# Strassen's scheme for the gates and the output product of a transformer block, in one item loop with the hidden layer

## The chip, the cores and the metric

One core of a Trainium2 chip. The metric is the device time of one execution, in microseconds; the median of several runs is given. The engines are TensorE (PE in the rows, with PEld for its weight loads), VectorE (DVE), ScalarE (ACT), GpSimd (POOL) and SyncE (SP), which here issues nearly all DMA transfers, in order.

## The reference

One block over 2048 latent tokens with 1024 channels, all in fp32. What matters here, cut down:

```python
q, k, v, p, g = split(modulate(layernorm(x)) @ w_in)
attn_d = banded_attention(q, k, v, ...) @ w_attn_branch
pooled = multiscale_pool(p)          # 4 groups of 128 channels, windows 2, 4, 8, 16, minus the token
pool_d = einsum('blgc,gcd->blgd', pooled, w_pool) * pool_scale
g_attn, g_pool = g[..., :1024], g[..., 1024:]
merged = sigmoid(g_attn) * attn_d + sigmoid(g_pool) * pool_d
x = layernorm(ALPHA * x + g1 * (merged @ w_out), ln1_g, ln1_b)
h = square(relu(modulate(layernorm(x)) @ w_mlp_in)) @ w_mlp_out
out = layernorm(ALPHA * x + g2 * h, ln2_g, ln2_b)
```

## The kernel before

fp32 products are made of three fp32r products: each operand is split into a rounded high part (ScalarE, line 59) and the rest (VectorE, line 62), and high x high, high x low and low x high are summed in PSUM. The channels u of the normalised, modulated input and the attention output lie channel-major in DRAM (`u_scr`, `a_scr`). TensorE's order is written by hand in attention and in both layers of the MLP; everything else, and all of TensorE's work in the stretch between them, is ordered by a scheduler that follows a simulated timeline.

Stages: the start and attention, up to 872 us; at its end the high and low parts of u for the first 1024 tokens are loaded (`load_u`) and two of the four pooling groups are computed between attention's products (`early_pool`). Then a stretch that runs once for each half of the tokens (`for c in range(2)`), to 1763 us: pooling channels (`p_group`: 8 x 3 x 3 matmuls of 344 columns), window sums on GpSimd (`p_finish`), the pooling branch's gate and map (`pool_gate`), the attention branch's gate (`sa`), the branch map with the merge (`mg`), and the output product token-major (`out_mm`: 256 columns each, 24 matmuls), with LN1 (`ln_affine`), a second normalisation (`ln1_u`) and the transposes back to channels (`u2_half`). u2_half also forms the four sums of half-size blocks that the hidden layer needs and stores seven planes in `us_scr`. All full products here take 24 matmuls of 512 columns for 128 channels x 512 tokens. 16 column pieces of w_ada are multiplied along the way (`ada_load`, `ada_sum`).

The hidden layer (`Pair`, from 1763 us) uses Strassen's scheme in Winograd's form: a 256-channel x 1024-token piece is cut 2 x 2, its 4-step sums are made on GpSimd, and seven products of half-size blocks (ORDER, 12 matmuls each) stand for eight. `step` splits the weights seven products ahead, `l_fill` splits the planes of the tokens. The outputs are combined with additions from PSUM on VectorE and four more sums on GpSimd, and go to DRAM (`hs_scr`) as planes for the second layer (`w2_fill`, `h_fill`, `prod2`, from 2393 us), which works in the same way and ends with LN2.

## Time and profile before

| | us |
|---|---|
| median of 3 runs | 3035.51 (3033.14 to 3039.31) |
| the profiled execution | 3039.96 |
| its span, first to last instruction | 3038.2 |
| start and attention | 872.3 |
| pooling, gates, branch map, output product, LN1 | 890.5 |
| hidden layer | 617.7 |
| between the layers | 12.5 |
| second layer and LN2 | 645.2 |

Of the span TensorE is busy for 2909.0 us, VectorE for 1819.1, ScalarE for 1369.1 and GpSimd for 1380.6. The stages are read off the first and last matmuls on each stage's PSUM tiles. In the rows below, "idle before" is the time in which the engine sat idle just before instructions of that group, and behind the arrow stands what ended most of it.

### The profile page before, as it was taken

To read this page: it belongs to the slowest core of one execution; us is meant where nothing else is said; L and a number is where in the kernel's file an instruction comes from. 1 tells how busy PE (TensorE), PEld (TensorE's weight loads), DVE (VectorE), ACT (ScalarE), POOL (GpSimd) and SP (SyncE) were. 2 spreads that over 40 slices of the span, in tenths; PEclk is the share of its full clock that TensorE was granted. 3 is DMA by queue.
4 is the path that set the end of the run, shared out by engine and by line. 5 is a ranking of instruction groups with operands and counts; after the bars stand their busy time and mean duration, and the time that the engine had idled before them with its cause. 6 is when DMAs were issued, how large, how long until landed. Compare 5 with 4: busy or idle time off the path is not lost. (4 is left out here: it accounts for less than half of the span.)

```text
span 3038.2 us, 42601 instructions
## 1 busy us (share of the span) xinstructions
PE 2909.0 (96%) x15336; PEld 2481.3 (82%) x15336; DVE 1819.1 (60%) x3201; ACT 1369.1 (45%) x2462; POOL 1380.6 (45%) x1638
## 2 busy tenths in 40 slices
PE   8899999999899999899999779999999799999998
PEld 5789989998888888888889668888888587888886
DVE  5577877877875444742144775557555453556675
ACT  3477767777741131432121455556555332333342
POOL 1867777777540014423032556657665240123244
PEclk9999999999999999999999889999999899999999
DMA  7111111112234433342122475547554684566563
GB/s 255 35 32 37 32 37 31 38 42 61 67 100 144 127 125 111 112 144 78 56 97 84 141 263 161 153 149 222 156 153 124 246 308 153 187 215 218 196 209 108
DMA packets 343015, 395.38 MB, mean 130 GB/s; under 512 B 16785, under 2 KB 277009, under 8 KB 341010
## 3 DMA queue, kind: packets, MB, share of 16 engines
q1 hardware_dynamic: 342802, 392.64, 40.5%
q8 instruction: 121, 1.98, 0.3%
q14 instruction: 92, 0.75, 0.1%
HBM read 275.13 MB, written 117.44 MB: 129 GB/s over the span
## 5 line engine op out<-in xcount | busy, mean ns | idle before, releaser
L1220 PE MATMUL ps_y<-La,R 128*128 128x512 f32 x2688 | 619.4, 393 | 25.8 <-ACT R L59 12.1
L1220 PEld LDWEIGHTS ps_y<-La,R 128*128 128x128 f32 x2688 | 508.9, 190 | 136.4 <-ACT La L59 13.7
L1039 PE MATMUL ps_h<-La,R 128*128 128x512 f32 x2112 | 485.2, 390 | 0.3 <-ACT cx L1044 0.3
L1039 PEld LDWEIGHTS ps_h<-La,R 128*128 128x128 f32 x2112 | 397.2, 188 | 83.3 <-ACT cx L1044 0.7
L62 DVE TENSOR_TENSOR R<-hraw,R 128x512 fp32r<-128x512 f32 x224 | 198.0, 890 | 150.7 <-ACT R L59 150.2
L59 ACT CAST R<-hraw 128x512 fp32r<-128x512 f32 x224 | 137.6, 621 | 281.3 <-PE ps_y L1220 272.9
L62 DVE TENSOR_TENSOR pl<-ps_pt,ph 128x512 fp32r<-128x512 f32 x312 | 212.5, 686 | 70.5 <-ACT ph L59 68.6
L465 POOL TENSOR_SCALAR s<-s,sm 128x640 f32<-128x640 f32 (+1 forms) x256 | 201.6, 795 | 103.0 <-DVE sm L464 53.9
L462 ACT ACTIVATE s<-s,sm 128x641 f32<-128x641 f32 (+1 forms) x256 | 209.8, 820 | 70.2 <-DVE sm L456 69.8
L456 DVE CUSTOM_DVE_ANT_0 s<-ps_s,mask,nsink 128x640 f32<-128x640 f32 (+1 forms) x256 | 211.5, 863 | 29.8 <-PE ps_s L451 29.7
L59 ACT CAST ph<-ps_pt 128x512 fp32r<-128x512 f32 x312 | 179.3, 580 | 109.3 <-PE ps_pt L486 106.0
L861 POOL TENSOR_TENSOR sa<-sa,m 128x512 f32<-128x512 f32 x32 | 57.1, 1805 | 374.5 <-DVE sa L860 374.5
L486 PE MATMUL ps_pt<-ident,s 128*128 128x128 f32 x1248 | 189.7, 274 | 12.4 <-DVE pl L62 8.2
L62 DVE TENSOR_TENSOR R<-sraw,R 128x512 fp32r<-128x512 f32 x160 | 146.3, 917 | 77.3 <-ACT R L59 76.8
L59 ACT CAST wh<-raw 128x2048 fp32r<-128x2048 f32 (+1 forms) x38 | 67.0, 1771 | 276.1 <-DMA raw<-w_in 73.6
L486 PEld LDWEIGHTS ps_pt<-ident,s 128*128 128x128 f32 x1248 | 151.6, 141 | 43.1 <-DVE pl L62 11.3
L62 DVE TENSOR_TENSOR wl<-raw,wh 128x2048 fp32r<-128x2048 f32 (+1 forms) x38 | 86.3, 2274 | 159.5 <-ACT wh L59 159.5
L59 ACT CAST R<-sraw 128x512 fp32r<-128x512 f32 x160 | 98.9, 621 | 155.2 <-PE ps_h L1039 97.5
L1039 PE MATMUL ps_h<-Lb,R 128*128 128x512 f32 x576 | 139.5, 396 | 25.4 <-ACT Lb L59 21.9
L1039 PEld LDWEIGHTS ps_h<-Lb,R 128*128 128x128 f32 x576 | 109.8, 191 | 49.7 <-ACT Lb L59 22.3
L66 PE MATMUL ps_out<-wh,mg 128*128 128x256 f32 x512 | 143.1, 281 | 0.0
L67 PE MATMUL ps_out<-wl,mg 128*128 128x256 f32 x512 | 142.8, 280 | 0.0
(264 smaller groups left out, 7098.4 us busy)
## 6 DMA issues: line engine op xcount, KB each, us to landing
hraw<-hs_scr SPq DMA_DIRECT2D x112, 512.0 KB, 4.0
w<-w_mlp_out SPq DMA_DIRECT2D x72, 512.0 KB, 5.4
sraw<-w_mlp_in SPq DMA_DIRECT2D x64, 512.0 KB, 6.3
hs_scr<-s SPq DMA_DIRECT2D x96, 256.0 KB, 4.6
raw<-w_in SPq DMA_DIRECT2D x19, 1024.0 KB, 5.5
raw<-w_ada SPq DMA_DIRECT2D x16, 1024.0 KB, 5.3
rw<-us_scr SPq DMA_DIRECT2D x14, 1024.0 KB, 5.4
raw<-u_scr SPq DMA_DIRECT2D x8, 1032.0 KB, 5.5
```

The lines of the kernel that those rows point to most:

```text
L59: act.copy(hi, src)
L62: (lo_eng or dve).tensor_tensor(lo, src, hi.bitcast(F32), ALU.subtract)
L66: pe.matmul(ps, sh, mh, start=first, stop=False)
L67: pe.matmul(ps, sh, ml, start=False, stop=False)
L456: dve.tensor_tensor_reduce(out=s[:, 0:n], in0=pieces[z][2], in1=mk[z], op0=ALU.add, op1=ALU.min, scale=-1.0 / math.sqrt(HD), scalar=nsink[ ...
L462: act.activation(s[:, 0:n + 1], s[:, 0:n + 1], AF.Exp, bias=sm[:, 0, j:j + 1], scale=-1.0, accum_out=sm[:, 1, j:j + 1])
L465: pool.tensor_scalar(s[:, 0:n], s[:, 0:n], sm[:, 2, j:j + 1], 1.0, ALU.mult, ALU.mult)
L486: pe.transpose(pt[:, c:c + P], self.s.probs[2 * z + j][:, o:o + P], ident)
L861: pool.tensor_tensor(s, s, m0[j][:, a:a + m], ALU.add)
L1039: pe.matmul(ps, a, b, start=p in (1, 6, 5) and k == 0 and i == 0, stop=k == 3 and i == 2, skip_group_check=p not in (1, 6, 5))
L1220: pe.matmul(ps, a, b, start=n == 0 and z == 0, stop=n == 15 and z == 2)
```

## The change

- **Pooling first.** All six remaining pooling groups of both halves are computed straight after attention, in an order of TensorE written by hand, and the pooled map times `pool_scale` goes to DRAM (`pd_scr`, `p_out`). `load_u` also forms four sums of u's half-size blocks in place on GpSimd (`act_sums`) and stores them (`us1`); the other three planes are read from `u_scr`.
- **Items.** Branch map, gates, output product and hidden layer are classes with the same methods, run in one loop whose order of products is written out: 8 `BranchCols` (plain products, to `ab_scr`), 16 `GateCols` (256 channels of one gate for one half of the tokens: seven products, sigmoid, multiplication with the loaded branch, and in the second of a pair the sum of both and the planes of the merged tensor to `ms_scr`), 8 `Rows` (the output product of 256 tokens, seven products of 512 columns, residual, LN1 in the first four), and 32 `HiddenCols`. Token-side planes of the next stage are loaded and split during the items ahead of it (`Stage.fill`).
- **LN1.** For the first half of the tokens it is done at the end of the item; for the second the sums go to DRAM and come back during the hidden layer of the first half (`ln1_late`). The transposes (`turn_pair`) stand in TensorE's order six to nine products behind.
- **Weights.** w_out times the gate g1 is formed on VectorE and stored as seven planes (`wo_scr`). The modulation's weights are multiplied on ScalarE and summed on VectorE.
- The second layer takes 1 MB tiles of the hidden planes in two buffers and splits its weight planes in halves.

```diff
+    def act_sums(v, sums, c, kk, e):
+        v = v.rearrange("p k (b r t) -> p k r b t", r=2, t=P)
+        a11, a12, a21, a22 = v[:, 0, 0], v[:, 1, 0], v[:, 0, 1], v[:, 1, 1]
+        e.tensor_tensor(a21, a11, a21, ALU.subtract)
+        e.tensor_tensor(a22, a22, a21, ALU.subtract)
+        e.tensor_tensor(a12, a12, a22, ALU.subtract)
+        e.tensor_tensor(a11, a11, a22, ALU.add)
+        for p, t in ((5, a11), (6, a22), (7, a21), (3, a12)):
+            sp.dma_start(sums[c][:, SPL[p], kk].rearrange("p (b t) -> p b t", t=P), t)
...
+            act_sums(raw[:, :, 8 * sums:8 * sums + CH], us1, sums, kk, pool)
...
+    def p_out(c, g, pooled):
+        (ph, pl), (wh, wl) = pooled
+        for jj in range(2):
+            j = 2 * g + jj
+            o = plp.tile([P, CH], F32, name="pdo", tag="pdo", bufs=2)
+            cc = slice(jj * P, (jj + 1) * P)
+            for a, n in HALF:
+                pd = ps2("ps_pd")
+                mm3(pd, (wh[:, cc], wl[:, cc]), (ph[:, a:a + n], pl[:, a:a + n]), True, True)
+                dve.tensor_scalar(o[:, a:a + n], pd, pscale[:, j:j + 1], None, ALU.mult)
+            for r in range(2):
...
+    pw = pool_w(2)
+    fin = [p_finish(early[0], 0, 0)]
+    groups = [(0, 2), (0, 3)] + [(1, g) for g in range(4)]
+    outs = [(0, 0)]
+    uu = uu0
+    for i, (c, g) in enumerate(groups):
+        if (c, g) == (1, 0):
+            uu = []
+            run(load_u(RA, CH - 8, uu, sums=1))
+        nw = pool_w(groups[i + 1][1]) if i + 1 < len(groups) else None
+        pt = p_group(uu, c, g, pw)
+        pw = nw
+        p_out(*outs.pop(0), fin.pop(0))
+        if i == 0:
+            fin.append(p_finish(early[1], 0, 1))
+            p_out(0, 1, fin.pop(0))
+        fin.append(p_finish(pt, c, g))
+        outs.append((c, g))
+    p_out(*outs.pop(0), fin.pop(0))
+    plx.close()
     ptx.close()
-    rpx.close()
...
+    rring = mpa.ring(6 * 4096, name="R")
...
+    rawring = mb.ring(3 * 8192, name="sraw")
+    rwring = mb.ring(3 * 2048, name="rw")
+    string = mb.ring(14 * 2048, name="st")
+    ldring = gp_[0].ring(4 * 2048, name="ld")
+    sring = gp_[0].ring(4 * 2048, name="s")
...
+    class Stage:
+        def __init__(self, src, L=None):
+            self.src, self.L = src, L or {}
+        def fill(self, p):
+            if p in self.L:
+                return
+            self.L[p] = []
+            for k in range(4):
+                raw = rwring.tile([P, 512], F32, name="rw")
+                s = self.src(p)[:, k]
+                sp.dma_start(raw if len(s.shape) == 2 else blocks(raw), s)
+                t = ltile(p, k)
+                split(t[:, 0], t[:, 1], raw)
+                self.L[p].append(t)
...
+    def combine(key, t, got, put, e=pool):
+        got[key] = t
+        add, sub = ALU.add, ALU.subtract
+        if key == 11:
+            put(1, t)
+        elif key == 22:
+            put(4, t)
+        elif key == 21:
+            s1, s2 = stile("s1"), stile("s2")
+            e.tensor_tensor(s1, t, got[22], add)
+            e.tensor_tensor(s2, s1, got[11], sub)
+            e.tensor_tensor(t, got[11], t, sub)
+            got["s2"] = s2
+            put(5, s1)
+            put(6, s2)
+            put(7, t)
+        else:
+            put(2, t)
+            s4 = stile("s4")
+            e.tensor_tensor(s4, t, got["s2"], sub)
+            put(3, s4)
...
+        def begin(self):
+            self.got, self.o = {}, {}
+        def put(self, p, t):
+            sp.dma_start(ms_scr[self.c][:, :, POS[p], self.n, :], blocks(t))
+        def fin(self, key, ps, t):
+            r, h = rn(key)
+            b = ldtile("br")
+            sp.dma_start(b, self.scr[:, 2 * self.n + h, self.c, r])
+            if t is None:
+                t = sttile("c11")
+                act.activation(t, ps, AF.Sigmoid)
             else:
+                dve.tensor_tensor(t, ps, t, ALU.add)
+                act.activation(t, t, AF.Sigmoid)
+            dve.tensor_tensor(t, t, b, ALU.mult)
+            self.o[key] = t
+            if self.other:
+                pool.tensor_tensor(t, t, self.other.o[key], ALU.add)
+                combine(key, t, self.got, self.put)
...
+    def ln1_rows(ts, b):
+        g, bb = ln1r
+        mu, rs = ln_root(mb, st1[:, b], "z")
+        nm = norm_bias(mu, rs)
+        for n, t in enumerate(ts):
+            cc = slice(n * 512, (n + 1) * 512)
+            if n == 0:
+                act.activation(t, t, AF.Identity, scale=rs, bias=nm)
+                pool.tensor_tensor(t, t, g[:, cc], ALU.mult)
+                pool.tensor_tensor(t, t, bb[:, cc], ALU.add)
+            else:
+                dve.scalar_tensor_tensor(t, t, mu, g[:, cc], op0=ALU.subtract, op1=ALU.mult)
+                dve.scalar_tensor_tensor(t, t, rs, bb[:, cc], op0=ALU.mult, op1=ALU.add)
+            sp.dma_start(x1_scr[b * P:(b + 1) * P, cc], t)
+            dve.bn_stats(st1[:, b, n, :], t)
+        mu, rs = ln_root(mb, st1[:, b], "z")
+        nm = norm_bias(mu, rs)
+        for t in ts:
+            act.activation(t, t, AF.Identity, scale=rs, bias=nm)
...
+    def turn_pair(i, kp, te, to):
+        c, bp = i // 4, i % 4
+        ps = ps2("ps_u2", "u", 2)
+        q = gp_[0].tile([P, 8, P], F32, name="u2q", tag="u2q", bufs=2)
+        for two in range(2):
+            k = 2 * kp + two
+            for r, ts in enumerate((te, to)):
+                pe.transpose(ps[:, (2 * two + r) * P:(2 * two + r + 1) * P], ts[k // 4][:, (k % 4) * P:(k % 4 + 1) * P], ident)
+            o = q[:, 2:6:3] if two else q[:, 0:8:7]
+            act.activation(o, blocks(ps[:, 256 * two:256 * two + 256]), AF.Identity,
+                           scale=mod[:, 32 + k, 0:1], bias=mod[:, 24 + k, 0:1])
+        a11, s2, a12, s3, s1, a22, s4, a21 = (q[:, z] for z in range(8))
+        pool.tensor_tensor(s1, a21, a22, ALU.add)
+        pool.tensor_tensor(s2, s1, a11, ALU.subtract)
+        pool.tensor_tensor(s3, a11, a21, ALU.subtract)
+        pool.tensor_tensor(s4, a12, s2, ALU.subtract)
+        sp.dma_start(us2[c][:, :, kp, bp * P:(bp + 1) * P], q[:, 0:7])
...
+            if t is None:
+                t = sttile("c11")
+                dve.scalar_tensor_tensor(t, xr, ALPHA, ps, op0=ALU.mult, op1=ALU.add)
+            else:
+                dve.tensor_tensor(t, ps, t, ALU.add)
+                dve.scalar_tensor_tensor(t, xr, ALPHA, t, op0=ALU.mult, op1=ALU.add)
+            dve.bn_stats(st1[:, b, h, :], t)
+            if self.n >= 4:
+                sp.dma_start(x1_scr[b * P:(b + 1) * P, cc], t)
+                return
+            self.rows[r, h] = t
+            if len(self.rows) == 4:
+                ts = [[self.rows[r, h] for h in range(2)] for r in range(2)]
+                for r in range(2):
+                    ln1_rows(ts[r], 2 * self.n + r)
+                for kp in range(4):
+                    ends.append((6 + kp, lambda kp=kp: turn_pair(self.n, kp, *ts)))
...
+        for k in range(KT):
+            act.mul(raw[:, k, :], raw[:, k, :], cs[:, k, 0:1])
+        dve.tensor_tensor(raw[:, 0:4], raw[:, 0:4], raw[:, 4:8], ALU.add)
+        dve.tensor_tensor(raw[:, 0:2], raw[:, 0:2], raw[:, 2:4], ALU.add)
+        dve.tensor_tensor(acc, raw[:, 0], raw[:, 1], ALU.add)
...
+    def w_out_planes(j):
+        raw = raw3([P, 2, D])
+        sp.dma_start(raw, w_out.rearrange("(k two p) n -> p k two n", two=2, p=P)[:, j])
+        dve.tensor_tensor(raw, raw, gb.unsqueeze(1).broadcast_to([P, 2, D]), ALU.mult)
+        b11, b12, b21, b22 = [raw[:, k, h * 512:(h + 1) * 512] for k in range(2) for h in range(2)]
+        t1, t2, t4 = (sring.tile([P, 512], F32, name="wt") for _ in range(3))
+        dve.tensor_tensor(t1, b12, b11, ALU.subtract)
+        dve.tensor_tensor(t2, b22, t1, ALU.subtract)
+        dve.tensor_tensor(b12, b22, b12, ALU.subtract)
+        dve.tensor_tensor(t4, b21, t2, ALU.subtract)
+        for p, t in ((1, b11), (6, t2), (2, b21), (7, b12), (5, t1), (4, t4), (3, b22)):
+            sp.dma_start(wo_scr[:, POS[p], j], t)
...
+    for k, i in enumerate((0, 1, 2, 2, 3, 4, 4, 5, 15, 17, 19, 21)):
+        job(i, ada, k)
+    for kk in range(4):
+        job(7 + 2 * kk, w_out_planes, kk)
...
+    job(24, to_rows)
+    for z in range(4):
+        job(33 + 2 * z, ln1_late, 4 + z)
+        job(42 + 2 * z, ada, 12 + z)
...
+    AHEAD = 5
...
+    for n, (p, i) in enumerate(seq):
+        for f in [f for d, f in ends if d == 0]:
+            f()
+        ends[:] = [(d - 1, f) for d, f in ends if d]
+        for j in at_step.get(n, ()):
+            ahead = [g for g in groups if g[0] == j + 1 + isinstance(items[j], BranchCols)]
+            for i2 in ahead[0] if ahead else ():
+                if i2 > 1:
+                    items[i2].load()
+                items[i2].begin()
+            for f in jobs.get(j, ()):
+                f()
+        if n + 11 < len(seq) and isinstance(items[seq[n + 11][1]], Rows):
+            items[seq[n + 11][1]].fetch(seq[n + 11][0])
+        items[i].prod(p)
+        for s, q in fills.get(n, ()):
+            s.fill(q)
+        if n + AHEAD < len(seq):
+            q, j = seq[n + AHEAD]
+            items[j].prep(q)
```

## Rows read from the trace of the kernel before

**Rows 1.** The page's engines: busy us, share of the span, instructions.
```profile
PE 2909.0 (96%) x15336; PEld 2481.3 (82%) x15336; DVE 1819.1 (60%) x3201; ACT 1369.1 (45%) x2462; POOL 1380.6 (45%) x1638
```

**Rows 2.** Busy time by stretch; columns in the first row, x counts instructions.
```profile
core 0: us, PE busy (x) PEld busy (x) DVE busy (x) ACT busy (x) POOL busy (x), PEclk, DMA share, GB/s
...
872.30:1762.80 890.50, 840.25 (x4545) 725.18 (x4545) 431.87 (x744) 237.69 (x344) 241.61 (x169) 0.97 0.36 118
...
1531.00:1619.50 88.50, 88.50 (x385) 71.94 (x384) 36.48 (x38) 19.52 (x25) 37.76 (x17) 1.00 0.31 103
1619.50:1711.00 91.50, 91.50 (x776) 91.43 (x775) 60.55 (x155) 23.25 (x40) 22.83 (x14) 1.00 0.15 58
1711.00:1763.00 52.00, 13.69 (x61) 9.17 (x59) 23.18 (x50) 22.22 (x36) 38.97 (x45) 0.59 0.78 258
1762.80:2380.50 617.70, 613.96 (x2687) 506.96 (x2688) 357.01 (x408) 329.31 (x534) 367.74 (x248) 0.99 0.54 165
2380.50:2393.00 12.50, 0.41 (x2) 0.00 (x0) 1.92 (x2) 2.94 (x5) 4.80 (x4) 0.60 0.76 243
```

**Rows 3.** TensorE's waits, 860 to 1800 us: in total, times, longest.
```profile
PE ps_h L1039 <- ACT Lb L59: 21.9, 1, 21.9
PE ps_u L929 <- ACT xn L900: 11.2, 3, 5.0
PE ps_u L929 <- ACT u2f L930: 9.3, 10, 2.1
PE ps_p L686 <- DVE ul L62: 4.7, 1, 4.7
```

**Rows 4.** TensorE's groups, whole span: busy us, mean ns, idle before and releaser.
```profile
L929 PE MATMUL ps_u<-ident,xn 128*128 128x128 f32 x128 | 25.0, 330 | 20.6 <-ACT xn L900 11.2 <-ACT u2f L930 9.3
```

**Rows 5.** GpSimd's groups in the hidden layer, dearest and cheapest of 512 elements.
```profile
L1066 POOL TENSOR_TENSOR s<-s,c 128x512 f32<-128x512 f32 x31 | 53.2, 1716 | 2.4
L1010 POOL TENSOR_TENSOR ext<-sraw,ext 128x512 f32<-128x512 f32 x30 | 40.8, 1358 | 51.0 <-DVE R L62 50.5 <-DMA sraw<-w_mlp_in 0.4
```

**Rows 6.** VectorE's groups, 872 to 1763 us.
```profile
L62 DVE TENSOR_TENSOR mg<-sa,mg 128x512 fp32r<-128x512 f32 x32 | 34.2, 1069 | 28.1 <-ACT mg L59 25.9
...
L88 DVE BATCH_NORM_STATS2 st<-acc 128x6 f32<-128x512 f32 x32 | 21.8, 685 | 2.2 <-POOL acc L911 2.1
...
L908 DVE SCALAR_TENSOR_TENSOR acc<-acc,mv,lnp 128x512 f32<-128x512 f32 x16 | 18.9, 1182 | 0.0
L62 DVE TENSOR_TENSOR pol<-po,poh 128x1024 fp32r<-128x1024 f32 x8 | 16.4, 2056 | 3.4 <-ACT poh L59 3.4
...
L910 DVE SCALAR_TENSOR_TENSOR acc<-acc,mv,lnp 128x512 f32<-128x512 f32 x16 | 13.5, 844 | 0.0
L97 DVE SCALAR_TENSOR_TENSOR mv<-mv 128x1 f32<-128x1 f32 x32 | 13.2, 413 | 1.3 <-ACT mv L95 1.3
```

**Rows 7.** GpSimd's groups, 840 to 1763 us: first and third level of window sums.
```profile
L767 POOL TENSOR_TENSOR ws<-pt 128x1039 f32<-128x1039 f32 x8 | 17.7, 2210 | 14.6 <-ACT pt L759 14.6
...
L771 POOL TENSOR_TENSOR ws<-ws 128x1033 f32<-128x1033 f32 x4 | 9.7, 2420 | 1.7 <-DVE pol L62 1.6
```

**Rows 8.** VectorE's groups in the hidden layer.
```profile
L62 DVE TENSOR_TENSOR R<-sraw,R 128x512 fp32r<-128x512 f32 x158 | 143.7, 912 | 53.3 <-ACT R L59 52.8
L62 DVE TENSOR_TENSOR R<-ext,R 128x512 fp32r<-128x512 f32 x63 | 76.1, 1209 | 64.1 <-ACT R L59 64.1
...
L1054 DVE TENSOR_TENSOR cv<-ps_h,cx 128x512 f32<-128x512 f32 x32 | 22.1, 690 | 21.6 <-PE ps_h L1039 21.1 <-issue 0.4
```

**Rows 9.** VectorE's groups in the second layer: splits of contiguous tiles.
```profile
L62 DVE TENSOR_TENSOR R<-hraw,R 128x512 fp32r<-128x512 f32 x224 | 198.0, 890 | 150.7 <-ACT R L59 150.2
```

**Rows 10.** Timelines of VectorE and GpSimd: start us, us, engine, idle before.
```profile
2202.08 0.69 DVE L62 TENSOR_TENSOR R<-ext,R 128x512 fp32r<-128x512 f32 x1
...
2213.44 1.70 DVE L62 TENSOR_TENSOR R<-ext,R 128x512 fp32r<-128x512 f32 x1 [2.50 <-ACT R L59]
...
2213.32 1.28 POOL L1020 TENSOR_TENSOR sraw<-sraw,ext 128x512 f32<-128x512 f32 x1
```

765 lines of the change are left out of this document (368 added, 397 removed).

## The prediction

> **What bounds the kernel now.** I read the page's engine shares first: TensorE is busy for 96% of the span [rows 1], so a saving counts only if it takes matmuls or TensorE's idle time away. Then the busy time by stage [rows 2]: the change rewrites the stretch from 872.3 to 1762.8 us (pooling, gates, branch map, output product, LN1). It lasts 890.5 us with TensorE busy for 840.25, so 50.2 us are idle; VectorE is busy there for 432 us, ScalarE and GpSimd for about 240 each. Third, TensorE's waits [rows 3] say where the 50.2 us lie: at the end, where the last LN1 rows, the transposes and the first planes of the hidden layer come one after another (1711 to 1763 us, 13.69 busy of 52, mean granted clock 0.59), and between the two halves of the tokens (u2f, ul). The hidden layer behind it, which already runs by seven products of half-size blocks, is busy for 613.96 of 617.7 us at 58% VectorE and 60% GpSimd; the changed stages take its form, so its rows are the price list for them.
>
> **TensorE's work, removed and added.** In the pure branch-map stretch, 385 matmuls of 512 columns fill 88.5 us: 0.230 us each [rows 2]. The gates have 2 halves x 16 channel tiles x 2 x 24 = 1536 of these. In the new form an item (128 x 2 channels, 1024 tokens) has 7 products x 4 x 3 = 84, and 16 items have 1344: 192 fewer, **-44.1 us**. The output product has 1536 matmuls of 256 columns; in its stretch 776 matmuls fill 91.5 us, 0.118 each, 181.1 us in all. Its 8 new items have 672 of 512 columns, 154.5 us: **-26.6**. The pooling (432 of 344 columns, 96 of 512 for its map), the branch map (768) and the 128 transposes [rows 4] keep their number and only move; half of the transposes now lie among the hidden layer's products. Together -70.7.
>
> **Idle time, removed and added.** The 50.2 us go, since the new order has another consumer ready wherever the old one had none: the last four output items and then the hidden items of the first half cover LN1 of the second. What comes instead:
>
> - Start of the pooling: the first weight tile is loaded and split just as before, 2.5 us. Before it, the sums of the first half (16 GpSimd operations of 512 elements, at 1.3 to 1.7 us [rows 5]) are queued between the softmax's normalisations and hold the two raw buffers longer, by four operations, some 5 us, for each of the last two loads; the early pooling's products lie among attention's, which can go on meanwhile. I take 3 us (0 to 10).
> - Load of the second half's u, in the pooling: the tiles fall free as the previous group's products run; each of the 4 loads then needs split, four GpSimd sums in place and four stores before its buffer is loaded again. GpSimd has 16 x 1.3 = 21 us for that, in line with the window sums of two groups. The load without the sums already cost 4.7 us at one point [rows 3]; I take 8 (4 to 20).
> - Pooling to branch map: TensorE's order is now written out, and the last map waits for the last group's window sums: four levels of 2.2 to 2.4 us on GpSimd [rows 7] and a split of 2.06 on VectorE [rows 6], some 12.5 us with the step between and without ScalarE's copies, against 2.8 us of other products. The 16 token tiles behind it go through three small buffers which lie on memory that the pooling gives up only then. 18 us (8 to 30).
> - Gates. An item gives TensorE 84 x 0.230 = 19.3 us. VectorE has per item 7 splits and 4 multiplications with two operands in SBUF, and 5 additions from PSUM at 0.690. The hidden layer's mix of splits, five at 0.912 and two at 1.209 [rows 8], is 0.997; so 11 x 0.997 + 3.45 = 14.4 us. The next stage's planes are split in two of the eight pairs, 56 tiles, 3.5 us per item on the mean; three jobs of w_out's planes and four of the modulation add some 30 us, 1.9 per item (estimated by tile size). 19.8 against 19.3: level on the mean, over it where the planes fall. 16 x 0.5 = 8 us (0 to 60, by the lowest and highest price of a split below).
> - Output items. VectorE per item: 7 splits at 0.89 [rows 9], 2 + 4 operations from PSUM at 0.69, 3 residuals at 0.84, 4 statistics at 0.685: 15.6 us. The first four items also have LN1 of two rows: per row 1.18 + 0.84, two statistics, and two roots of small operations whose longest takes 0.41 [rows 6], 6.4 us, so 12.8 per item. That makes 28.4 us against TensorE's 19.3 + 16 x 0.195 = 22.4: 24 us too much in four items. The last pair also splits the hidden layer's planes (28 x 0.89 = 25): 56 against 38.6. The two items between give back 7, the five products of lead 14. LN1 is awaited by TensorE itself: the transposes stand in its order six products (16.6 us) behind the item, and whatever is queued behind them waits too. The first pair ends both items at once, 25.6 us of LN1 in those 16.6. I take 25 us (5 to 45).
>
> Sum of new idle: 2.5 + 3 + 8 + 18 + 8 + 25 = 64.5. The second-layer stage keeps its products; its loads are now 1 MB in two buffers for 512 KB in three, its splits twice as many and half as long, and the 12.5 us ahead of it are bound by the same loads, which I leave at zero change (-8 to +8). Loss at the lower clock is left as it is inside the old 840.25.
>
> The profiled execution took 3039.96 us, 1.8 more than its span. 3039.96 - 70.7 - 50.2 + 64.5 = 2983.6; the median of the runs is 4.45 us under the profiled execution, so **2979 us**, 1.9% less.
>
> **A row that speaks against it.** VectorE and GpSimd get in each other's way: the split that starts at 2213.44 takes 1.70 us, and it ends 0.54 us after the GpSimd addition that began before it at 2213.32 and took 1.28; the same split at 2202.08, with GpSimd idle, took 0.69 [rows 10]. The two means of the splits [rows 8] lie between these ends. The Trainium skill, page "SBUF — State Buffer", section "SBUF: two separate sides", says that the port pair these two share is an exclusive lock held for a whole instruction, and that the loser blocks; the trace agrees, 1.70 against 0.69. Priced by the rows, a pair of gate items has 16 GpSimd operations of 1.29 and on the mean 29 VectorE ones of 0.69: 20.6 + 20.0 = 40.6 us against 38.6, if none of it can overlap: 16 us in eight pairs, where the sum above has 8.
>
> **Rivals.**
> - All hidden: the non-PE queues are ordered by the scheduler, which may put LN1 behind the splits, and the lead of five products absorbs the bursts. New idle 15 to 20: 2930 us. For it: the hidden layer hides the same kind of burst at its own middle. Against it: VectorE at over 100% in six output items. Chance 0.25.
> - The exclusive pair decides: gates and output items run at the sum of both engines. 2 us x 8 pairs by the count above, up to 26 us at a mean price of 1.07 (row of mg [rows 6]) with its waits in the output items: 3000 to 3025 us, say 3010. For it: the rows of the split; against it: in the hidden layer 357 + 368 busy us fit into 617 with no wait. Chance 0.14.
> - Slower: VectorE becomes the bound of all gate items. Each has 14.5 operations of the kind that blocks, and 5.35 us of others. Up to 3042 us there are 63 from my forecast, which with my 8 are 71 / 16 = 4.4 us per item, 23.7 = 14.5 x + 5.35: from x = 1.27 us on it is slower, and at 1.4 it gives 3072 us. The dearer row of splits has 1.209 [rows 8]. Chance 0.07.
> - The gap in front of the hidden layer stays, because its planes wait for the last transposes: 38 us back, 3017. Four output items (77 us) lie between, so 0.04.
>
> **How the numbers follow.** Forecast 0.50, all hidden 0.25, pair 0.14, gap 0.04, slower 0.07. The range takes in the all-hidden case with a better joint ahead of the second layer and the pair's upper end: 2920 to 3025. The bound of "same" is 0.2%, 6 us, about what a measurement of this kernel can tell from no change: 3029 to 3042. Faster 0.89, same 0.04, slower 0.07.
>
> **What would show it.** Right: 512-column matmuls of gates and output at 0.230 us and 2016 of them; no idle stretch of 30 us ahead of the hidden layer; TensorE waits of some 18 us between pooling and branch map, and of 20 to 30 at the transposes and splits of the output items, with VectorE over 90% busy there. Wrong: VectorE splits in the gates dearer than 1.1 us on the mean; waits behind loads, which I count as free; idle over 20 us ahead of the second layer.

## The result and the profile after

The changed kernel takes 3262.21 us (median of 4 runs, 3257.03 to 3266.58), the kernel before beside it 3036.95 (3033.14 to 3039.31): the ratio is 1.0742, 95% interval 1.0721 to 1.0763. It is 7.4% slower, where 1.9% faster was forecast; the time lies 283 us above the forecast.

The page of the kernel after: busy us, share and instructions of the engines, then TensorE's busy tenths and granted clock in 40 slices.

```profile
PE 2941.7 (90%) x14280; PEld 2423.8 (74%) x14280; DVE 2095.7 (64%) x3534; ACT 1641.8 (50%) x3069; POOL 1541.4 (47%) x1822
...
PE   8899999997975998879967987799999798999998
...
PEclk9999999998986999999988999999999898999999
```

TensorE has fallen from 96% to 90% of a longer span, and its busy time grew by 33 us [rows 1] although it has 70.7 us less work at full clock. Both point the same way: it waits, and part of what it does is done at a lower clock. VectorE is 277 us busier and GpSimd 161. The next view is the busy time by stage, of the kernel after (columns as in rows 2; the stretches are pooling, branch map, gates, output product, hidden layer first and second half, gap, second layer):

```profile
880.80:1028.20 147.40, 106.57 (x528) 97.00 (x528) 84.00 (x92) 34.11 (x53) 68.41 (x42) 0.83 0.55 161
1028.20:1237.00 208.80, 192.00 (x793) 150.54 (x794) 81.57 (x118) 87.58 (x174) 13.38 (x8) 0.92 0.65 202
1237.00:1620.70 383.70, 334.12 (x1361) 262.59 (x1360) 295.23 (x337) 152.14 (x282) 180.15 (x114) 0.95 0.64 193
1620.70:1858.40 237.70, 181.98 (x737) 141.90 (x736) 158.14 (x314) 126.55 (x208) 75.29 (x94) 0.89 0.63 198
1858.40:2253.80 395.40, 339.96 (x1416) 265.52 (x1415) 240.31 (x370) 232.98 (x416) 222.69 (x198) 0.96 0.61 185
2253.80:2572.30 318.50, 312.85 (x1347) 251.81 (x1345) 180.10 (x204) 159.96 (x268) 188.55 (x128) 1.00 0.49 147
2572.30:2585.60 13.30, 0.03 (x1) 0.03 (x1) 2.04 (x4) 3.10 (x6) 4.33 (x4) 0.69 0.81 260
2585.60:3251.90 666.30, 639.15 (x2688) 513.28 (x2688) 393.58 (x572) 256.75 (x417) 174.35 (x93) 0.97 0.58 200
```

The table sets each stretch against its work, which is the number of matmuls times the 0.230 us (or the share of it by columns) of [rows 2], with the transposes and the modulation's products. What is over that is idle time or lower clock.

| stage | length | work | over it | forecast |
|---|---|---|---|---|
| start and attention (before: 872.3) | 880.8 | 872.3 | 8 | 3 |
| pooling | 147.4 | 90 | 57 | 10.5 |
| branch map | 208.8 | 180 | 29 | 18 |
| gates | 383.7 | 310 | 74 | 8 |
| output product, LN1 | 237.7 | 162 | 76 | 25 |
| hidden layer, first half | 395.4 | 317 | 78 | 0 |
| hidden layer, second half | 318.5 | 309 | 10 | 0 |
| second layer (before: 633.0) | 666.3 | 633.0 | 33 | 0 |

With 2 us of gap and tail that is 367 us against 64.5. The difference, 302, less 19 that the forecast's work contained beyond the column "work" (among it the old losses at a lower clock, "left as it is"), is the 283 us. The last 26 us of the pooling row (1002 to 1028.2) are its joint with the branch map, which the forecast has under the branch map: TensorE waits 9.4 us there for the last group's window sums and 10.4 for the first token tile. The second layer of the kernel before, for comparison:

```profile
2393.00:3026.00 633.00, 619.28 (x2688) 508.89 (x2688) 375.11 (x516) 213.16 (x331) 174.71 (x93) 0.98 0.63 212
```

Which engine TensorE waits for in the gates, and what ScalarE waits for there (kernel after, 1237 to 1611 us; us in total, times, longest):

```profile
PE ps L882 <- ACT cx L886: 22.1, 6, 7.4
PE ps L882 <- DVE cv L894: 7.9, 4, 3.9
PE ps L882 <- DVE cv L1034: 6.7, 4, 2.3
PE ps L882 <- DVE R L66: 6.6, 6, 2.9
```

```profile
ACT cx L1035 <- DVE cx L1034: 27.8, 10, 5.6
ACT cu L1035 <- DVE cu L1034: 24.8, 12, 2.5
```

Most of the waits are no waits for a split: they end with a copy or sum that reads a PSUM bank out (L886, L894, L1034) before the next product writes to it. ScalarE's copies are queued behind sigmoids (L1035), and these wait for VectorE. ScalarE also waits 44.0 us there for weights from memory, its longest item; but experiment 3 below, in which the stage is 59 us shorter, still has 35.4 of these. VectorE is only 77% busy in the stage, but its operations are long. Its groups of the gates in the kernel after (busy, mean ns of one, idle before and releaser):

```profile
L66 DVE TENSOR_TENSOR R<-sraw,R 128x512 fp32r<-128x512 f32 x81 | 80.5, 996 | 20.3 <-ACT R L63 20.2
L1036 DVE TENSOR_TENSOR cv<-cv,br 128x512 f32<-128x512 f32 x16 | 23.0, 1437 | 0.7 <-ACT cv L1035 0.7
L1036 DVE TENSOR_TENSOR cu<-cu,br 128x512 f32<-128x512 f32 x14 | 22.5, 1610 | 0.0
L889 DVE TENSOR_TENSOR cu<-ps,cx 128x512 f32<-128x512 f32 x16 | 10.9, 682 | 0.5 <-DMA ms_scr<-cx 0.5
```

The last row reads from PSUM and costs 0.68, as its like do in [rows 8] (0.69); three of the four multiplications per item, which the forecast priced like the splits at 0.997, cost 1.44 to 1.61. One chain of it, from the timelines of GpSimd, VectorE and TensorE (start us, us, engine, idle before):

```profile
1399.21 1.59 POOL L948 TENSOR_TENSOR s<-cx,cv 128x512 f32<-128x512 f32 x1
1400.88 1.61 POOL L949 TENSOR_TENSOR s<-s,c 128x512 f32<-128x512 f32 x1
```

```profile
1399.60 1.75 DVE L66 TENSOR_TENSOR R<-ext,R 128x512 fp32r<-128x512 f32 x1
1401.27 1.77 DVE L1036 TENSOR_TENSOR cu<-cu,br 128x512 f32<-128x512 f32 x1
```

```profile
1401.40 2.60 PE L882 MATMUL ps<-La,R 128*128 128x512 f32 x10 [2.86 <-DVE R L66]
1405.45 5.81 PE L882 MATMUL ps<-La,R 128*128 128x512 f32 x24 [1.45 <-ACT cx L886]
```

GpSimd's addition ends at 1400.80 and the split at 1401.35, 0.55 us behind it; the next one ends at 1402.49 and the multiplication at 1403.04, again 0.55 behind: the pattern of [rows 10]. TensorE stands for 2.86 us until that split is through. The next wait of 1.45 us is for a copy that ScalarE had behind a sigmoid, and that behind 3.31 us of the modulation's products (L1179). A wait can also cost clock: of 1455 to 1465 us the windows show

```profile
1455.00:1465.00 10.00, 5.98 (x17) 4.82 (x18) 8.24 (x12) 5.29 (x10) 4.97 (x4) 0.51 0.81 241
```

and TensorE's timeline in it

```profile
1459.02 5.49 PE L882 MATMUL ps<-La,R 128*128 128x512 f32 x12 [6.71 <-ACT cx L886]
```

12 matmuls in 5.49 us, 0.458 each, twice the 0.230 from [rows 2]: behind 6.71 us without work the granted clock is at the lower of its two levels, 1.2 of 2.4 GHz. By the trace's clock records the kernel before is at that level 12 times for 128 us in all, the kernel after 41 times for 293 us.

### The profile page after: what moved, and what is told of

Its sections match the earlier page's. It is cut to its first block, busy times and chain, and to the rows that moved or that the text cites. A ratio compares the mean times of both kernels' runs of the same rounds, so it can differ in the third digit from the quotient of the medians.

```text
span 3264.8 us, 42936 instructions
## 1 busy us (share of the span) xinstructions
PE 2941.7 (90%) x14280; PEld 2423.8 (74%) x14280; DVE 2095.7 (64%) x3534; ACT 1641.8 (50%) x3069; POOL 1541.4 (47%) x1822
## 3 DMA queue, kind: packets, MB, share of 16 engines
q1 hardware_dynamic: 478080, 495.96, 48.6%
## 5 line engine op out<-in xcount | busy, mean ns | idle before, releaser
L882 PE MATMUL ps<-La,R 128*128 128x512 f32 x4704 | 1148.7, 405 | 85.7 <-ACT cx L886 38.4
L882 PEld LDWEIGHTS ps<-La,R 128*128 128x128 f32 x4704 | 903.3, 194 | 316.9 <-ACT cx L886 45.9
L1427 PE MATMUL ps_y<-La,R 128*128 128x512 f32 x2688 | 639.2, 400 | 40.4 <-ACT La L63 26.8
L66 DVE TENSOR_TENSOR R<-sraw,R 128x512 fp32r<-128x512 f32 x328 | 314.5, 961 | 96.1 <-ACT R L63 95.6
L63 ACT CAST R<-sraw 128x512 fp32r<-128x512 f32 x328 | 200.8, 617 | 266.5 <-PE ps L882 173.7
L920 POOL TENSOR_TENSOR ext<-sraw 128x512 f32<-128x512 f32 x48 | 70.9, 1478 | 366.1 <-DMA sraw<-w_in 265.1
L66 DVE TENSOR_TENSOR La<-rw,La 128x512 fp32r<-128x512 f32 x172 | 137.2, 809 | 72.1 <-ACT La L63 71.2
L63 ACT CAST La<-rw 128x512 fp32r<-128x512 f32 x172 | 104.4, 619 | 154.1 <-DMA rw<-us 81.0
L70 PE MATMUL ps_ab<-La,R 128*128 128x512 f32 x256 | 105.2, 411 | 26.3 <-ACT La L63 26.3
L506 PE MATMUL ps_o<-ph,vring 128*128 128x256 f32 x368 | 118.2, 336 | 4.9 <-ACT o L515 4.9
L66 DVE TENSOR_TENSOR R<-ext,R 128x512 fp32r<-128x512 f32 x96 | 86.8, 904 | 48.2 <-ACT R L63 48.1
```

What stands on the lines that cost most here:

```text
L63: act.copy(hi, src)
L66: (lo_eng or dve).tensor_tensor(lo, src, hi.bitcast(F32), ALU.subtract)
L70: pe.matmul(ps, sh, mh, start=first, stop=False)
L506: pe.matmul(self.po[:, z * 256:(z + 1) * 256], v, self.p[u][w][:, x * 256:(x + 1) * 256], start=w == 0 and mine[0] == (z, i), stop=w == 1 ...
L882: pe.matmul(ps, a, b, start=first and k == 0 and i == 0, stop=k == 3 and i == 2, skip_group_check=not first)
L920: pool.tensor_tensor(self.op[5], b12, b11, ALU.subtract)
```

## The experiments

Each is the kernel after with the edit shown. Totals are single times unless an interval stands with them; the stretches are those of one profiled execution. Stages that an edit does not touch move too, since the other engines' order is scheduled anew: the gates take 372 to 384 us in the kernels that change nothing in them (the kernel after, 7 and 8; the kernel after is the longest). Smaller differences there are not read.

**1. Loads, first question: is it the one DMA queue?** The branch's loads left out (another tile in memory multiplied in), and the second layer's loads back to 512 KB.

```diff
-            b = ldtile("br")
-            sp.dma_start(b, self.scr[:, 2 * self.n + h, self.c, r])
+            b = gb[:, 0:512]
...
-    hring = m2p.ring(2 * 8192, name="hraw")
+    hring = m2p.ring(3 * 4096, name="hraw")
```

> Two edits in stages that follow one another, each read from its own stage. Gates (374 us in the changed kernel, 310 without waits): the branch is not loaded, the sigmoid is multiplied with a tile that is there; the multiplication stays. This leaves out the branch's value. Second layer (666 us): hidden planes are loaded as 512 KB halves in three buffers, as before. Theory Q (the one in-order DMA queue: loads through shallow rings wait for VectorE to free a slot, and what is queued behind them, weights and planes, comes late; ScalarE waits for it with PSUM copies behind): gates 325 to 340 us, second layer 635 to 645. Rival V (VectorE and GpSimd share one way to SBUF and are full): gates 365 or more, since the operations stay. Rival B (bandwidth): 45 of 189 GB/s are gone in the gates, 350 to 360; second layer unchanged, 660 to 670.

3246.86 us. Windows of gates and second layer in this run:

```profile
1237.00:1612.00 375.00, 329.78 (x1362) 258.92 (x1362) 292.09 (x336) 151.55 (x281) 179.53 (x114) 0.97 0.50 155
2570.70:3232.10 661.40, 638.86 (x2688) 513.13 (x2688) 390.34 (x571) 257.54 (x417) 174.23 (x93) 0.97 0.60 202
```

The DMA share falls from 0.64 to 0.50, the gates stay in that range: these loads on the queue are not the cause. The smaller tiles give back 5 of the second layer's 33 us.

**2. The sums of u, and the branch loaded but not read.** The second edit keeps the loads and takes the wait for their buffers away.

```diff
-        e.tensor_tensor(a21, a11, a21, ALU.subtract)
-        e.tensor_tensor(a22, a22, a21, ALU.subtract)
-        e.tensor_tensor(a12, a12, a22, ALU.subtract)
-        e.tensor_tensor(a11, a11, a22, ALU.add)
...
-            dve.tensor_tensor(t, t, b, ALU.mult)
+            dve.tensor_tensor(t, t, gb[:, 0:512], ALU.mult)
```

> Gates: the branch is loaded as in the changed kernel, into the same ring and by the same queue, but the multiplication reads another tile, so that a load waits for no operation of VectorE; the branch's value is left out. Pooling (147.5 us, 90 of work): the four sums of u on GpSimd are left out, their stores stay. Theory Q: gates as in the run without these loads, within 8 us. Rival B (bandwidth, or the number of transfers): gates stay at 365 to 380. Pooling: if the sums in place hold the raw buffers, 125 to 135 us, otherwise 143 to 150.

3244.30 us. Pooling and gates:

```profile
868.10:1007.50 139.40, 98.12 (x529) 90.33 (x529) 75.32 (x92) 33.93 (x53) 43.35 (x27) 0.86 0.63 185
1222.30:1606.00 383.70, 333.78 (x1362) 261.50 (x1362) 296.31 (x338) 152.31 (x281) 179.00 (x114) 0.95 0.51 158
```

The gates are the same to 0.1 us. But as nothing held them, the loads ran ahead, from 983 us on: the DMA share of the gates falls to 0.51 as in 1, and the branch map's rises from 0.65 to 0.78. So this is a second test of the gates without these loads, not one with their traffic kept. The start shrinks from 880.8 to 868.1 (12.7, more than the excess of 8.5 over the kernel before) and the pooling by 8.0, although the wait at its end for the first token tile grows from 10.4 to 17.6 us beside the early loads; so the sums of u may be worth more than 8 there. The branch map gives 6 back (214.9).

**3. GpSimd out of the gates, LN1 out of the output items.** GpSimd's sums of the weight blocks and of the merged gates are left out, and LN1 of the first half.

```diff
-                pool.tensor_tensor(t, t, self.other.o[key], ALU.add)
-                combine(key, t, self.got, self.put)
+                for p in {11: (1,), 22: (4,), 21: (5, 6, 7), 12: (2, 3)}[key]:
+                    self.put(p, t)
...
-                    ln1_rows(ts[r], 2 * self.n + r)
```

> Gates: all of GpSimd's operations are left out (block sums of weights and outputs, the merge), the DMA transfers and VectorE's and ScalarE's operations stay. Output product (238 us, 162 of work): LN1 of the first four items is left out, transposes and stores stay. Rival V: gates 325 to 335 us, since VectorE's splits fall from 0.95 to 0.69 us. Theory Q: 355 or more. Output product: if LN1's burst on VectorE and the wait for it is what TensorE loses there, 185 to 195 us; if it is the chain of the transposes themselves and the loads, 215 to 235.

3157.34 us. Gates and output product, then two of VectorE's groups in the gates:

```profile
1237.10:1562.10 325.00, 316.82 (x1361) 254.51 (x1360) 218.23 (x341) 155.79 (x284) 0.00 (x0) 0.99 0.73 228
1562.10:1751.20 189.10, 167.74 (x737) 133.37 (x736) 116.07 (x182) 73.97 (x129) 41.07 (x72) 0.99 0.77 243
```

```profile
L66 DVE TENSOR_TENSOR R<-sraw,R 128x512 fp32r<-128x512 f32 x113 | 77.6, 687 | 28.9 <-ACT R L63 28.6
L1039 DVE TENSOR_TENSOR cv<-cv,br 128x512 f32<-128x512 f32 x16 | 11.0, 687 | 0.9 <-ACT cv L1038 0.7
```

The gates lose 58.7 us, the output product 48.6. VectorE does the same work in 218 us instead of 295: 77 us of its busy time were being blocked. TensorE's idle time goes from 49.6 to 8.2 and its busy time for the same 1361 matmuls from 334.1 to 316.8: 41.4 us of waits and 17.3 of lower clock. Bandwidth is no bound either: at 0.73 the DMA share is higher in the faster kernel.

**4. Two other suspects:** the modulation on VectorE instead of ScalarE, and the transposes spread in TensorE's order.

```diff
-                    ends.append((6 + kp, lambda kp=kp: turn_pair(self.n, kp, *ts)))
+                    ends.append((8 + 2 * kp, lambda kp=kp: turn_pair(self.n, kp, *ts)))
...
-            act.mul(raw[:, k, :], raw[:, k, :], cs[:, k, 0:1])
...
+            dve.scalar_tensor_tensor(acc, raw[:, k, :], cs[:, k, 0:1], acc, op0=ALU.mult, op1=ALU.add)
```

> Branch map (208.8 us, 180 of work): the products with the modulation's weights go back from ScalarE to VectorE. If ScalarE, waiting for these weights in its order, holds up the token splits behind it, the branch map falls to 185 to 192 us; if the token tiles' loads alone are late, it stays at 203 to 212. Output product and hidden layer, first half (238 and 366 us): the four groups of transposes of an item stand two products apart instead of one, the first of them two products later (one in the hidden layer). If TensorE's waits there are for the two PSUM tiles and two buffers behind each group (26.6 and 26.3 us), both stages fall by 20 to 35 us; if LN1 itself is late, by less than 12.

3261.23 us. The branch map takes 206.2 us instead of 208.8: ScalarE's wait for the modulation's weights is not what holds its splits up. Output product and first half of the hidden layer:

```profile
1602.90:1833.80 230.90, 179.17 (x737) 140.08 (x736) 156.23 (x314) 124.03 (x207) 74.42 (x95) 0.90 0.64 203
1833.80:2247.20 413.40, 347.80 (x1416) 271.85 (x1415) 248.81 (x388) 220.08 (x381) 220.83 (x198) 0.93 0.59 176
```

7 us less in the one, as if LN1 itself were late there; 18 more in the other, which neither theory had. In the hidden layer the two edits meet (part of the modulation is done there, with 18 more instructions on VectorE), so the 18 us cannot be put down to the transposes alone.

**5. Time on the engines, or the chain of steps?** GpSimd's operations in the gates keep number, order and waits but work on an eighth of the elements; so do LN1's large operations on VectorE.

```diff
+                n = slice(0, 64)
+                pool.tensor_tensor(t[:, n], t[:, n], self.other.o[key][:, n], ALU.add)
...
-                dve.scalar_tensor_tensor(t, t, mu, g[:, cc], op0=ALU.subtract, op1=ALU.mult)
+                dve.scalar_tensor_tensor(t[:, 0:64], t[:, 0:64], mu, g[:, 512:576], op0=ALU.subtract, op1=ALU.mult)
```

> Leaving out all of GpSimd's operations brought the gates from 384 to 325 us. Here they all stay, in number, order and waits, on 64 of their 512 elements (so the sums are left out for the rest). Theory V (their time on the way to SBUF that VectorE shares holds VectorE up): 325 to 338 us. Rival C (others wait for GpSimd's results, or for its place in the order): 365 to 384. Output product (238 us) and hidden layer, first half (395 us): of LN1 the two operations of VectorE per half row and the statistics run on 64 of 512 elements, all other steps and waits stay. If VectorE's time decides: 205 to 215 and 370 to 380 us; if the chain of many small steps that TensorE's transposes wait for decides: 228 to 238 and 388 to 395.

3189.37 us. Gates, output product, first half of the hidden layer:

```profile
1234.40:1560.70 326.30, 318.39 (x1361) 255.55 (x1360) 219.87 (x341) 155.99 (x285) 53.41 (x114) 0.99 0.73 226
1560.70:1783.70 223.00, 177.33 (x738) 139.61 (x737) 136.63 (x309) 123.79 (x204) 67.75 (x94) 0.91 0.64 204
1783.70:2178.40 394.70, 341.56 (x1415) 267.66 (x1414) 214.53 (x370) 232.96 (x417) 223.20 (x198) 0.95 0.62 187
```

All 114 operations and their waits are there, and the stage is as short as without them: the length of GpSimd's operations costs the 57 us (46 against the shortest of the unchanged stages, 372), not the mere step through GpSimd. Whether somebody waits for their results that long, or whether they hold VectorE up, is asked in 9. In LN1 it is the other way round: the output product takes 223.0, 15 of the 49 us, and the hidden layer's first half 394.7, none. TensorE's waits for LN1's last step on ScalarE stay too, 19.8 us in the output product where the kernel after has 23.0. So LN1's price goes mostly with the rest of its chain, and with the place in TensorE's order where the transposes wait for it; the small steps and the operations on ScalarE and GpSimd, which keep their length here, are not told apart.

**6. GpSimd's work in the gates awaited by nobody, the second layer's weight sums neither stored nor read again.**

```diff
-                pool.tensor_tensor(t, t, self.other.o[key], ALU.add)
-                combine(key, t, self.got, self.put)
+                pool.tensor_tensor(gscr, gscr, gscr, ALU.mult)
...
-            sp.dma_start(t3_scr[:, jj], t)
```

> Gates: GpSimd has as many operations of the full 512 elements as in the changed kernel, at the same places of the order, but on a tile of its own for which nobody waits; the sums themselves are left out. Theory V: 370 to 390 us, as in the changed kernel. Rival C: 325 to 338, as with none of them. Second layer (666 us; 633 in the kernel before): the two sums of weights that are stored and read again are neither stored nor read (plain blocks are read in their place). If loads of weights wait there for these stores' buffers: 640 to 650; otherwise 660 to 668.

3216.53 us. As nothing held them, the operations ran ahead of the gates and fell into the branch map. The question was not answered by that, but another was. Branch map, gates, second layer:

```profile
1028.80:1254.20 225.40, 196.82 (x793) 152.84 (x794) 123.10 (x120) 87.09 (x174) 143.30 (x114) 0.89 0.60 186
1254.20:1585.80 331.60, 317.53 (x1361) 254.24 (x1360) 218.05 (x340) 155.14 (x283) 0.00 (x0) 0.99 0.73 226
2545.60:3201.50 655.90, 634.34 (x2688) 509.78 (x2688) 392.02 (x572) 256.93 (x417) 177.17 (x93) 0.98 0.54 191
```

VectorE's splits of the token tiles in the branch map, first of the kernel after, then of this run:

```profile
L66 DVE TENSOR_TENSOR La<-rw,La 128x512 fp32r<-128x512 f32 x44 | 29.8, 690 | 27.8 <-ACT La L63 27.7
```

```profile
L66 DVE TENSOR_TENSOR La<-rw,La 128x512 fp32r<-128x512 f32 x44 | 51.2, 1192 | 13.2 <-ACT La L63 13.0
```

GpSimd work that has nothing to do with the branch map takes its splits from 0.690 to 1.192 us and the stage from 208.8 to 225.4, where VectorE has work for 39% of the time. The stores and their rereading are worth 10 us of the second layer; the kernel before has them too.

**7. LN1 out of both places; the window sums on 64 elements.**

```diff
-                pool.tensor_tensor(n[:, 1:PW], s[:, 0:PW - 1], s[:, 1:PW], ALU.add)
+                pool.tensor_tensor(n[:, 0:64], s[:, 0:64], s[:, 64:128], ALU.add)
...
-            ln1_rows(ts[r], b)
```

> LN1 is left out in both places (the first four output items, and the four pieces in the hidden layer's first half); loads, stores, transposes and the modulation behind them stay. Output product: 189 us as in the run that left it out there. Hidden layer, first half (395 us, 320 of work): if LN1 is what TensorE loses there: 335 to 345; if the transposes' own chain (PSUM tile, ScalarE, four sums, store) is: 370 to 390. Pooling (147.5 us, 90 of work): the window sums run on 64 of 1040 elements. If their levels on GpSimd are what the maps wait for: 120 to 128; if the second half's load is: 135 to 145.

3166.96 us. Pooling, output product, first half of the hidden layer:

```profile
881.50:1007.60 126.10, 99.39 (x528) 91.24 (x529) 66.02 (x91) 34.03 (x53) 33.16 (x40) 0.89 0.65 188
1592.10:1787.00 194.90, 172.41 (x737) 136.28 (x736) 121.84 (x180) 72.30 (x126) 51.48 (x78) 0.96 0.77 239
1787.00:2156.40 369.40, 331.18 (x1416) 262.51 (x1416) 199.53 (x248) 193.78 (x347) 198.93 (x183) 0.98 0.66 199
```

The window sums cost 21 us of the pooling; LN1 costs 26 of the hidden layer's first half and 43 of the output product. What stays there is in good part the transposes themselves: without LN1 TensorE still waits 19.3 us of the output product for the copies that empty their PSUM tiles, and 30.3 of the hidden layer's first half.

**8. The branch's stores on ScalarE's queue,** so that loads behind them on SP do not wait.

```diff
-                sp.dma_start(ab_scr[:, 2 * self.n + j, self.c, r, 256 * h:256 * h + 256].rearrange("p (b t) -> p b t", t=P), v[:, r])
+                act.dma_start(ab_scr[:, 2 * self.n + j, self.c, r, 256 * h:256 * h + 256].rearrange("p (b t) -> p b t", t=P), v[:, r])
```

> Branch map (208.8 us, 180 of work): its stores are issued from ScalarE's queue right behind the copy that they wait for, not from SyncE's, where they hold up the token tiles' loads behind them (SyncE waited 64 us for these copies). If the order of that queue is what delays the tokens: 188 to 196 us; if the three small buffers of the tokens are: 203 to 210.

3255.59 us, the branch map 209.3 instead of 208.8: the order of that queue costs nothing that can be read.

**9. GpSimd's operations full and in their place, results unread; no sums of the transposed groups** (the planes are stored in four pieces instead of one). What 6 was meant to ask.

```diff
+                pool.tensor_tensor(gscr, t, self.other.o[key], ALU.add)
+                self.got[key] = t
...
-        pool.tensor_tensor(s1, a21, a22, ALU.add)
-        pool.tensor_tensor(s2, s1, a11, ALU.subtract)
-        pool.tensor_tensor(s3, a11, a21, ALU.subtract)
-        pool.tensor_tensor(s4, a12, s2, ALU.subtract)
```

> Gates: GpSimd has as many operations of 512 elements as in the changed kernel, on the same inputs and so at the same times, but writes to a tile that nobody reads (the sums are left out of the planes). Theory V (their time on the shared way): 365 to 385 us. Rival C (somebody waits for their results): 325 to 340. Output product (238 us) and hidden layer, first half (395 us): the four sums on GpSimd of each transposed group are left out, LN1 stays, the store keeps its size. If these sums (64 of 128 elements per stage) are part of what TensorE's transposes wait for: 215 to 225 and 370 to 382 us; if not: 232 to 240 and 388 to 396.

3223.40 us. Gates and first half of the hidden layer:

```profile
1234.40:1600.50 366.10, 327.62 (x1361) 260.69 (x1361) 306.05 (x337) 151.78 (x281) 181.34 (x114) 0.96 0.64 200
1835.50:2214.30 378.80, 335.75 (x1416) 262.51 (x1415) 236.99 (x370) 233.70 (x418) 192.54 (x136) 0.97 0.64 193
```

The stage stays 41 us above experiment 3, 6 below the shortest unchanged one, though nobody waits for GpSimd's results, and VectorE is busy for 306 us with the work that takes 218 there. Only the buffers that GpSimd reads from are still held until it is done; a share of that is not told apart. The sums of the transposed groups cost 17 us in the hidden layer and none in the output product (235.0).

**10. The merge's sums on VectorE, no LN1, no sums of the transposed groups.**

```diff
-                pool.tensor_tensor(t, t, self.other.o[key], ALU.add)
-                combine(key, t, self.got, self.put)
+                dve.tensor_tensor(t, t, self.other.o[key], ALU.add)
+                combine(key, t, self.got, self.put, dve)
```

> Gates: the eight additions of the merge and of the output planes per pair of items go from GpSimd (1.29 us) to VectorE (0.69 us); nothing is left out there. Theory V, by the time on the shared way (35.8 us per pair instead of 40.6): 340 to 360 us, although VectorE gets 44 us more to do. A rival by which VectorE's own busy time decides: 390 to 410. Output product and hidden layer, first half: LN1 is left out in both places and the four sums of a transposed group too. Without LN1 alone they took 189 to 195 and 369 us. If the sums are the rest of the loss: 175 to 185 and 335 to 350; if not: 187 to 195 and 362 to 370.

3141.12 us. Gates, output product, first half of the hidden layer:

```profile
1237.20:1593.00 355.80, 325.63 (x1362) 258.31 (x1362) 288.14 (x394) 152.22 (x282) 89.33 (x56) 0.97 0.65 203
1593.00:1781.10 188.10, 168.35 (x738) 133.09 (x737) 118.55 (x187) 72.48 (x128) 12.21 (x8) 0.99 0.79 250
1781.10:2129.30 348.20, 326.31 (x1415) 259.15 (x1414) 201.15 (x249) 194.00 (x347) 166.35 (x119) 1.00 0.70 210
```

VectorE has 57 more instructions in the gates and is busy for 7 us less: half of GpSimd's operations less was worth more than their work costs there. The hidden layer's first half comes down by 47 us; of the 30 that it still has over the second half, 8 are the transposes' own time; the other 22 are TensorE's idle time (348.2 less 326.3), of which 18.3 are waits for the copies out of the transposes' PSUM tiles.

**11. Five small buffers instead of three** for the token tiles of the branch map (and twelve instead of fourteen elsewhere).

```diff
-    rwring = mb.ring(3 * 2048, name="rw")
-    string = mb.ring(14 * 2048, name="st")
+    rwring = mb.ring(5 * 2048, name="rw")
+    string = mb.ring(12 * 2048, name="st")
```

> The small buffers through which token tiles and planes are loaded are five instead of three, at the cost of two of the fourteen output buffers. Branch map (208.8 us): the run with the stores on another queue left it at 209, so the order of the queue was not it; if the depth of these buffers is: 190 to 198 us. If it is the lower clock after the gap ahead of it and the loads' own time, 203 to 209. The other stages: gates 372 to 385 by theory V, since the operations stay.

3235.82 us; the branch map takes 202.2, 6.6 less. That is a part of its 29.

**12. The repairs that keep the whole computation:** the merge's sums on VectorE (10), five buffers (11), 512 KB loads in the second layer (1).

> The whole computation, with three repairs together: the gates' merge and output planes on VectorE, five small buffers instead of three, hidden planes of the second layer as halves in three buffers. Theory V, from the stages of the single runs: gates 350 to 360 us, branch map 200 to 204, second layer 658 to 665; 3200 to 3230 us in all, still 5 to 6% over the kernel before, since LN1 and the transposes in the item loop (some 110 us) and the pooling (57) are not touched. If the repairs hide one another, 3235 to 3262.

3212.97 us (3212.80 to 3213.52), 1.0583 of the kernel before (1.0565 to 1.0601). The gates take 357.1, the branch map 202.0, the second layer 657.3. It is better than the kernel after by 49 us, and no version that computes everything beat the kernel before.

## Why the prediction was wrong, step by step

- **TensorE's work: right.** 2016 products of 512 columns at 0.230 us are what the gates and the output product cost TensorE: in experiment 3 it is busy for 317 and 168 us with 310 and 162 of work. The step that failed is the other one, "new idle 64.5".
- **Gates, 8 us (0 to 60): 74.** Here the cause is settled: with GpSimd short (5) or out of the stage (3) 57 to 59 us of it go (46 to 47 against the shortest unchanged stage), with its operations present and unread (9) only 18 (6), without the branch's loads in the stage (1, 2) none that can be read. The prediction saw the row that speaks against it [rows 10] and gave it the wrong measure: it compared VectorE's mean load per item with TensorE's, 19.8 against 19.3. The measured load is 295.23 / 16 = 18.5 us per item, so by that test the stage should be level. It takes 24.0. The mean is no test, because product, PSUM sum, sigmoid, multiplication and the next product's bank are one chain, in which a single operation blocked for 1 us moves TensorE. The rival "exclusive pair" had the mechanism and the price too low by the same habit (16 us). Its 29 VectorE operations per pair are what the trace has of the kind that blocks (234 splits and multiplications in eight pairs), but the stage has 337 / 8 = 42: the additions from PSUM, 10 per pair, which stand in the same queue, were left beside, and so were the waits that the chain makes of the blocking. The slower rival named the stage, but set its point at 1.27 us for an operation; the splits from `sraw` are at 0.996 on the mean, below it. "Splits dearer than 1.1" would not have shown the trouble; the multiplications at 1.44 to 1.61 did.
- **The rule weighed.** The Trainium skill, page "SBUF — State Buffer", section "SBUF: two separate sides", has the loser of the shared port pair block until the other's instruction ends. The trace agrees: the split and the multiplication above end 0.55 us behind GpSimd's additions, and in experiment 6 splits go from 0.690 to 1.192 us beside foreign GpSimd work.
- **Output items, 25 us (5 to 45): 76.** LN1 accounts for 43 to 49 of it (7, 3), and only 15 go with the length of VectorE's large operations (5). The prediction counted LN1 as VectorE load, 25.6 us for a pair against a lead of 16.6, and expected VectorE over 90% busy here; it is busy for 158 of 238 us, 67%. What it did not count is the latency of LN1's whole chain, which the transposes in TensorE's written order wait for, and the transposes' own stand: without LN1 the stage is still 27 us over its work, with 21.4 us of waits for their copies in experiment 3. The waits are in the trace of the output items (1611 to 1849 us), the first for the copies that empty the transposes' PSUM tiles, the second for LN1's last step on ScalarE (L1087):

```profile
PE ps_u L1097 <- ACT u2q L1099: 26.6, 16, 5.1
PE ps_u L1097 <- ACT cx L1087: 19.4, 3, 8.4
```

- **Hidden layer's first half, 0: 78.** `ln1_late` and the second half's transposes moved into this stage, and the prediction charged it nothing for them, on the ground that products cover them. They do not: TensorE's order is fixed there, so it stands at each group of transposes (26.3 us in 16 waits for the copies alone). LN1 is worth 26 (7), the sums of the transposed groups 17 (9), both together 47 (10); most of what is left are waits for the copies.
- **Pooling, 10.5: 57.** 20 of it are the two waits at the joint, which the prediction put under the branch map; 37 are the stage's own. Window sums are 21 (7), sums of u 8 or more (2); the rest is not taken apart. The prediction charged GpSimd's four levels to the last group alone, as part of the branch map's 18; the stage itself pays for them too. **Start, 3: 8.** The sums of u are worth 12.7 there (2).
- **Branch map with its joint, 18 (8 to 30): 29** in the stage, and 20 in the two waits ahead of it: together 49, above the bounds. Three small buffers are 6.6 (11), the store queue none (8), the modulation on ScalarE no more than 3 (4); the rest stays open.
- **Second layer, 0 (±8): 33.** For the same 2688 products TensorE is idle for 27.2 us instead of 13.7, and busy for 639.2 instead of 619.3: waits for splits of the weights, and the lower clock behind them. The 1 MB loads are 5 (1, and 9 with the other repairs of 12). The stores of weight sums (6) explain none of it, since the kernel before has them as well. Some 24 to 28 us are open.
- **"Loss at the lower clock is left as it is": wrong.** It was 12 stretches, 128 us, and became 41, 293 us. Where the products go on without a wait it goes too: the gates' granted clock is 0.99 in experiment 3 and 0.95 in the kernel after.

The forecast's sign rested on six idle terms, most of them nearer to the low end of their bounds. With the upper ends, 2.5 + 10 + 20 + 30 + 60 + 45 = 167.5 instead of 64.5, the time would have been 3082 and the sign the other one; the range stopped at 3025. Measured are 367, of which 121 lie in three stretches that were priced at zero. How the shares add up inside one stage is known only roughly, since each was taken out by itself.

## What to carry to other kernels

Where VectorE and GpSimd both work on tiles in SBUF during a stage bound by TensorE, do not compare mean loads: look for a chain product, PSUM copy, elementwise step, next product, and price each of its operations at its blocked length. Test it cheaply by shortening GpSimd's operations to an eighth with all waits kept: if the stage shrinks, and stays long with the operations at full length and their results unread, the blocking is the cause and not the wait for a result, and sums moved from GpSimd to VectorE can make VectorE less busy. And when an order of TensorE is written out by hand, a step of it that waits for another engine, such as a transpose behind LN, is not covered by the products behind it; price the latency of its whole chain, and count the clock that a wait can take afterwards.

## What was not expected of the hardware

- In the gates the time came near to the sum of what VectorE and GpSimd take undisturbed. VectorE alone takes 218 us there (3), GpSimd's 114 operations 143 (6), together 361: the stage takes 366 with the results unread and 372 to 384 with them. With 58 sums moved to VectorE it is 218 + 58 x 0.69 + 56 x 1.26 = 329 against 356, and in the branch map of experiment 6 82 + 143 = 225 against 225.4. No run shows that this sum is what sets the time, and the fit may be chance: by the start and end times in the traces neither of the two engines works for 71 of the 384 us in the gates of the kernel after, nor for 47 of the 225 us in that branch map. Operations that read PSUM keep their 0.68 us beside GpSimd.
- The blocking seems to go both ways: GpSimd's additions take 1.59 to 1.61 us in the chain above, where one in [rows 10] takes 1.28; its 114 operations take 180 us in the gates of the kernel after and 143 in experiment 6, 1.58 and 1.26 on the mean.
- Waits of a few us can be paid twice. In the gates 41.4 us of idle time came with 17.3 us of matmuls at a lower clock.
